# Reordered first loads, later decay tables, halved last sums and two-step sums of squares in a hybrid decoder layer

## The chip, the cores and the metric

The kernel runs on one core of a Trainium2 chip. The metric is device time in microseconds (us) of one execution. The core has five engines with their own instruction queues: TensorE (PE in the profile, with its weight loads shown apart as PEld), VectorE (DVE), ScalarE (ACT), GpSimd (POOL) and SyncE (SP), which here only issues DMAs. Each engine runs its queue in order; semaphores hold an instruction until what it depends on is done.

## The reference, cut to what matters

One decoder layer on x of shape (1, 1024, 1024), float32:

```python
xn   = rmsnorm(x, attn_norm_g)
proj = xn @ w_in                       # q, k, v of groups A and B, forget logits
qa, ka = rmsnorm(qa, q_norm_a), rmsnorm(ka, k_norm_a)       # per head of 64
out_a  = sliding_window_attention(qa, ka, va, sinks)        # 8 heads on 2 kv heads, window 128, ALiBi
qb, kb = rmsnorm(qb, q_norm_b), rmsnorm(kb, k_norm_b)
out_b  = forgetting_attention(qb, kb, vb, log_sigmoid(f + b_forget))   # 8 heads, causal
h = x + concat(out_a, out_b) @ w_out
y = h + relu(rmsnorm(h, mlp_norm_g) @ w_up) ** 2 @ w_down   # 4096 hidden
```

## The kernel before, in words

Everything is float32. A product of two float32 matrices is made of three matmuls in a faster float32 mode: each operand is split into a high part (a rounded copy, on ACT or DVE) and a low part (operand minus high part, on DVE or POOL; helper `split`, lines 74 to 79), and high·high, high·low and low·high are summed in PSUM. All matmuls come from the helper `mm` on line 72, so they share that line in the profile.

**Start (lines 166 to 204).** x comes transposed, 128 rows of it per step k = 0..7, each in two DMAs of 512 columns into `xr` (lines 177 and 181). The step's weights come as `wr`, 192 KB (line 178): by SP's queue, only for k = 0 by ACT's queue. DVE casts `wr` to the high part (line 78), DVE (k = 0) or POOL makes the low part (line 79); ACT scales x into `xh` (line 184), DVE makes `xl` (line 185). PE sums 24 products per step into eight PSUM banks `qps`, one per token tile t; the results are copied to `q0` by DVE (even t) and ACT (odd t) on line 203. Eight matmuls on a zero tile run before the first real one. `xr` has four buffers, shared later with `xq`; `wr` has three.

**Decay tables.** `ab` (lines 390 to 405) holds slope times distance for the 8 heads of group A: eight DVE multiplications of 128x256 of the tile `dist`, which POOL makes. They stand late in the program but need only `dist`, so they can be placed early in DVE's queue. They are read by the first scores of group A (line 506).

**Norms.** The second copy of x, `xq`, is squared and summed on ACT (line 379) for the row norms, which DVE and ACT turn into `rstd`, `ep2` and `rqk` (lines 380 to 385 with the helper `rsqrt`, lines 81 to 91). `qknorm` (lines 236 to 277) normalises queries and keys: POOL squares up to 1024 columns (line 244), one DVE instruction sums groups of 64 (line 249), small DVE and ACT steps make the factor (lines 254 to 269), POOL multiplies it in (line 275). It runs 14 times: ten with 16 groups, four with 12.

**Attention, then the two feed-forward products.** Projections of the next heads are matmuls that fill PE between scores (lines 501 to 510 and 652 to 661), transposed probabilities (`evict_pt`, lines 364 to 371: ACT makes `pth`, DVE then `ptl`) and sums with v. The feed-forward products use a seven-product scheme on half matrices; the loop `down` (lines 1124 to 1175) ends with product n = 2, whose four banks d = 0..3 are finished by DVE (lines 1226 and 1227: multiply by `rr`, add to a stored sum) and stored by SP one by one (line 1228).

**What sets the order.** A planner orders each engine's queue: it runs a cost model of the program in time and at each step issues, per engine, the ready instruction of the highest priority (program order, raised by `tc.high_priority(offset)` for `prep`, `load_w` and others). `tc.issue_after(ins)` adds one rule: what the block traces on `ins`'s engine is queued behind `ins`. Dependences between engines are kept by semaphores that the planner's framework sets per tile.

Of the kernel before, what the change touches and what calls it, by code (L numbers as in the profile page):

```python
# [12 lines left out]
ALU = mybir.AluOpType  # L13
# [3 lines left out]
P = 128  # L17
# [4 lines left out]
HD = 64  # L22
NH = 8
# [10 lines left out]
NU = 4  # L34
NS = 4
DEPTH = 2

LAST = (6, 7, 0, 1, 2, 3, 4, 5)
ORDER_B = (0, 2, 1, 3)
# [15 lines left out]
def hybrid_layer(  # L55
# [15 lines left out]
    def mm(out, lhsT, rhs, start, stop):  # L71
        return nc.tensor.matmul(out, lhsT, rhs, start=start, stop=stop)  # L72
# [101 lines left out]
    for k in range(KT):  # L174
        xr = ap2.tile([P, S], F32, tag="s", name="xr", bufs=NS)
        wr, wh, wl = w_tiles(384)
        nc.sync.dma_start(xr[:, halves[0]], xT[k * P : (k + 1) * P, halves[0]])
        (nc.sync if k else nc.scalar).dma_start(wr, w_a0[:, k, :])
        if k == 0:
            nc.scalar.preload_act_table_set("natural_log_exp_and_others")  # L180
        nc.sync.dma_start(xr[:, halves[1]], xT[k * P : (k + 1) * P, halves[1]])
        split(wh, wl, wr, nc.vector, nc.gpsimd if k else nc.vector)
        for cs in halves:
            nc.scalar.activation(xh[:, k, cs], xr[:, cs], AF.Copy, scale=ga[:, k : k + 1])
            nc.vector.scalar_tensor_tensor(
                out=xl[:, k, cs], in0=xr[:, cs], scalar=ga[:, k : k + 1],
                in1=xh[:, k, cs].bitcast(F32), op0=ALU.mult, op1=ALU.subtract,
            )
        passes = ((xh, wh), (xh, wl), (xl, wh))
        order = (  # L190
            [(t, j) for j in range(3) for t in range(NT)] if k == 0
            else [(t, j) for t in (range(NT) if k < KT - 1 else LAST) for j in range(3)]
        )
        for t, j in order:
            x_, w_ = passes[j]
            mm(
                qps[t][:, :384], x_[:, k, t * P : (t + 1) * P], w_,
                k == 0 and j == 0, k == KT - 1 and j == 2,
            )
# [36 lines left out]
    def qknorm(x, nh, tlo, thi, r=None):  # L236
# [9 lines left out]
            ap3.tile([P, 16], F32, tag=tag, name=tag, bufs=2)[:, : n * nh]  # L246
            for tag in ("ss", "sr0", "su")
        )
        nc.vector.tensor_reduce(
            out=ss, in_=sq[:, : n * w].rearrange("p (g d) -> p g d", d=HD),  # L250
            axis=AX.X, op=ALU.add,
        )
        th = lambda a: a.rearrange("p (t h) -> p t h", h=nh)
        nc.vector.scalar_tensor_tensor(
            out=th(ss), in0=th(ss), scalar=1.0 / HD,
# [145 lines left out]
        out=dist, in_=dist, pattern=[[1, 256]], compare_op=ALU.is_ge, fill=BIG,  # L401
        base=-1, channel_multiplier=-1,
    )
    for h in range(NH):
        nc.vector.tensor_scalar_mul(ab[h // 4][:, h % 4, :], dist, 2.0 ** -(h + 1))

    before = cp.tile([NH * NT, NH, NT], F32, name="before")
    nc.gpsimd.memset(before, 1.0)
# [715 lines left out]
    def down(i):  # L1124
# [8 lines left out]
        for ci in range(2):  # L1133
# [26 lines left out]
            for n in products:  # L1160
# [5 lines left out]
                split(w[:, 0], w[:, 1], src[n], nc.scalar, nc.vector if own else nc.gpsimd)  # L1166
                for d in range(4):
                    ds_ = slice(d * P, (d + 1) * P)
                    for k in range(2):
                        first, end = g + ci + k == 0, (g, ci, k) == (NG - 1, 1, 1)  # L1170
                        mm(ps[d], w[:, 0, k, ds_], x[:, 0, k], first, False)
                        mm(ps[d], w[:, 0, k, ds_], x[:, 1, k], False, False)
                        mm(ps[d], w[:, 1, k, ds_], x[:, 0, k], False, end)
                if (g, ci) == (NG - 1, 1):
                    finish(n, ps)

# [26 lines left out]
    def finish(n, ps):  # L1203
# [6 lines left out]
        for d in range(4):  # L1210
# [8 lines left out]
            elif n == 4:  # L1219
                plus(t[:, d], ps[d], sums["m7"][:, d])  # L1220
            elif n == 5:
                for name in ("m16", "m7"):
                    minus(sums[name][:, d], sums[name][:, d], ps[d])
            else:
                y = sums["m1"][:, d]
                nc.vector.tensor_tensor(out=ps[d], in0=ps[d], in1=rr[:, left], op=ALU.mult)
                plus(y, ps[d], y)
                nc.sync.dma_start(yT[d * P : (d + 1) * P, left], y)
        if n == 5:
            late.extend([("c21", 4, left), ("m7", 4, right), ("m16", 0, right)])  # L1230
        elif n == 3:
# [77 lines left out]
```

## Time and profile before

| | |
|---|---|
| time, median of 3 runs | 1115.2 us (1113.52 to 1115.54) |
| the profiled execution's own time | 1111.68 us |
| its span, first to last instruction | 1110.0 us |
| PE busy | 98% |
| DVE busy | 69% |
| ACT busy | 52% |
| POOL busy | 33% |
| mean granted TensorE clock | 0.999 of full speed |

A busy share is time in which at least one instruction of the engine ran. Matmuls are pipelined, so the distance between the starts of two of them (their pitch) is what one costs, and it is shorter than the duration shown. The end of a matmul is modelled.

### The profile page before, as it was taken

The numbers are of one execution on the slowest core, as the hardware profiler recorded it, in microseconds if no ns is written. First come the engines' busy times: TensorE is split into PE (matmuls) and PEld (weight loads), VectorE is DVE, ScalarE is ACT, GpSimd is POOL, SyncE is SP. The second block draws the span as 40 slices with busy tenths as digits, with TensorE's granted clock in tenths as the row PEclk, the third lists the DMA queues.
The fourth block names the chain that finished last, engine by engine and source line by source line (L and its number), as shares of the span: only waits on it lengthen the run. The fifth ranks groups of instructions, "written<-read, shape, count | busy, mean of one in ns | idle before, by whom it ended". The sixth has DMA issues, their size and how long they took to land.

```text
span 1110.0 us, 15616 instructions
## 1 busy us (share of the span) xinstructions
PE 1087.6 (98%) x5551; PEld 934.2 (84%) x5551; DVE 770.4 (69%) x1311; ACT 573.1 (52%) x1013; POOL 361.6 (33%) x338
## 2 busy tenths in 40 slices
PE   8999998999999999999999999999999999999998
PEld 7999987799997888787888888888888888888886
DVE  7476656765767477799868688756675877674395
ACT  5557657757667666555454535353443433333331
POOL 4662512424434655124322223322222222222100
PEclk9999999999999999999999999999999999999999
DMA  9301211304538566473554544334699786665423
GB/s 303 137 28 46 85 35 43 105 15 140 181 103 321 180 204 225 158 253 131 185 198 172 186 165 171 142 133 180 250 391 344 275 300 238 218 230 198 172 95 114
DMA packets 95935, 195.69 MB, mean 176 GB/s; under 512 B 7360, under 2 KB 19312, under 8 KB 95856
## 3 DMA queue, kind: packets, MB, share of 16 engines
q1 hardware_dynamic: 95568, 194.47, 49.9%
q8 instruction: 44, 0.72, 0.3%
q14 instruction: 35, 0.29, 0.1%
q10 hardware_dynamic: 288, 0.22, 0.1%
HBM read 141.61 MB, written 53.04 MB: 175 GB/s over the span
## 4 chain that ended last, share of the span: by engine, by line
PE 82%; DVE 9%; DMA 3%; issue 3%; ACT 2%; POOL 1%; SPq 0%; DVEq 0%; ACTq 0%; POOLq 0%
PE pd L72 27%; PE pu L72 26%; PE ps L72 12%; PE po L72 5%; PE spb L72 3%; PE pvb L72 3%; PE tpb L692 2%; PE sp L72 1%; DMA xq<-in_x_dram 1%; DVE ptl L368 1%; PE pv L72 1%; PE tpa L527 1%; DVE bl L79 1%; DVE sb L656 1%; DVE bl L918 1%
## 5 line engine op out<-in xcount | busy, mean ns | idle before, releaser
L72 PE MATMUL pd<-hx,wx 128*128 128x512 f32 x1344 | 304.8, 389 | 0.0
L72 PEld LDWEIGHTS pd<-hx,wx 128*128 128x128 f32 x1344 | 252.3, 188 | 52.4
L72 PE MATMUL pu<-bh,wu 128*128 128x512 f32 x896 | 276.6, 390 | 0.4 <-ACT wu L76 0.4
L72 PEld LDWEIGHTS pu<-bh,wu 128*128 128x128 f32 x896 | 168.2, 188 | 36.0 <-ACT wu L76 0.8
L72 PE MATMUL pu<-bl,wu 128*128 128x512 f32 x448 | 174.4, 390 | 0.8 <-DVE bl L79 0.8
L72 PE MATMUL ps<-w,xh 128*128 128x384 f32 (+1 forms) x640 | 173.4, 342 | 0.3 <-ACT qkb L609 0.3
L76 ACT CAST hx<-hr 128x1024 fp32r<-128x1024 f32 x56 | 59.0, 1054 | 175.8 <-PE pd L72 171.2
L79 POOL TENSOR_TENSOR wx<-wda,wx 128x1024 fp32r<-128x1024 f32 x24 | 64.4, 2684 | 196.5 <-ACT wx L76 188.1
L79 DVE TENSOR_TENSOR hx<-hr,hx 128x1024 fp32r<-128x1024 f32 x56 | 72.4, 1302 | 74.0 <-ACT hx L76 74.0
L72 PEld LDWEIGHTS ps<-w,xh 128*128 128x128 f32 x640 | 114.9, 189 | 1.3 <-ACT qkb L609 0.6
L72 PE MATMUL ps<-w,xl 128*128 128x384 f32 (+1 forms) x320 | 109.0, 341 | 0.0
L72 PEld LDWEIGHTS pu<-bl,wu 128*128 128x128 f32 x448 | 84.1, 188 | 18.9 <-DVE bl L79 1.4
L72 PE MATMUL po<-mix,wos 128*128 128x512 f32 x384 | 95.5, 396 | 0.7 <-ACT wos L76 0.7
L79 POOL TENSOR_TENSOR wu<-wus,wu 128x512 fp32r<-128x512 f32 x32 | 48.1, 1506 | 127.0 <-ACT wu L76 127.0
L72 PEld LDWEIGHTS po<-mix,wos 128*128 128x128 f32 x384 | 69.9, 188 | 14.5 <-ACT wos L76 1.1
L79 POOL TENSOR_TENSOR wu<-wur,wu 128x512 fp32r<-128x512 f32 x32 | 43.5, 1361 | 87.1 <-ACT wu L76 87.1
L368 DVE TENSOR_TENSOR ptl<-tpb,pth 128x512 fp32r<-128x512 f32 (+1 forms) x80 | 50.1, 633 | 29.8 <-ACT pth L367 29.2
L76 ACT CAST wu<-wus 128x512 fp32r<-128x512 f32 x64 | 38.4, 618 | 58.5 <-PE pu L72 56.0
L79 POOL TENSOR_TENSOR w<-wr,w 128x384 fp32r<-128x384 f32 (+1 forms) x47 | 50.0, 1079 | 49.3 <-ACT w L76 36.5
L987 DVE TENSOR_TENSOR ht<-hb 128x512 f32<-128x512 f32 x32 | 21.8, 722 | 63.4 <-ACT hb L1042 63.4
L76 ACT CAST wx<-wda 128x1024 fp32r<-128x1024 f32 x56 | 58.5, 1050 | 7.0 <-DMA wda<-in_w_d_dram 7.0
L367 ACT CAST pth<-tpb 128x512 fp32r<-128x512 f32 (+1 forms) x80 | 43.2, 544 | 34.7 <-PE tpb L692 30.1
(214 smaller groups left out, 1951.4 us busy)
## 6 DMA issues: line engine op xcount, KB each, us to landing
wda<-in_w_d_dram SPq DMA_DIRECT2D x34, 1024.0 KB, 8.8
hr<-hid_d SPq DMA_DIRECT2D x56, 512.0 KB, 6.1
wur<-in_w_u_dram SPq DMA_DIRECT2D x32, 512.0 KB, 4.3
hid_d<-ht SPq DMA_DIRECT2D x16, 1024.0 KB, 4.3
hid_d<-hb SPq DMA_DIRECT2D x16, 768.0 KB, 3.6
mix<-mixs_d SPq DMA_DIRECT2D x7, 1024.0 KB, 7.7
wr<-in_w_b_dram SPq DMA_DIRECT2D x32, 192.0 KB, 2.5
xr<-in_xT_dram SPq DMA_DIRECT2D x16, 256.0 KB, 4.3
```

The source lines that it names most:

```text
L72: return nc.tensor.matmul(out, lhsT, rhs, start=start, stop=stop)
L76: hi_eng.copy(hi, src)
L79: lo_eng.tensor_tensor(out=lo, in0=src, in1=hi.bitcast(F32), op=ALU.subtract)
L367: nc.scalar.copy(hi[:, cols], pt[:, cols])
L368: nc.vector.tensor_tensor(out=lo[:, cols], in0=pt[:, cols], in1=hi[:, cols].bitcast(F32), op=ALU.subtract)
L527: nc.tensor.transpose(tp[:, hh * P : (hh + 1) * P], pts[hh // 2][:, hh % 2, c0 : c0 + P], ident)
L656: nc.vector.tensor_tensor_reduce(out=pr[:, c * 512 : c * 512 + n], in0=sp[:, :n], in1=cb[:, c * 512 : c * 512 + n], scale=1.0, scalar=3e38 ...
L692: nc.tensor.transpose(tp[:, c0 : c0 + P], probs[qi][:, kb * P : (kb + 1) * P], ident)
L918: nc.vector.scalar_tensor_tensor(out=lo, in0=src, scalar=gain, in1=hi.bitcast(F32), op0=ALU.mult, op1=ALU.subtract)
L987: eng.tensor_tensor(out=out, in0=a, in1=b, op=ALU.subtract)
```

## The change

Four edits. The weights of step 0 are issued on SP's queue as its first DMA, ahead of the first half of x, instead of on ACT's queue behind `vecs`; the load of ACT's function table follows in the program. The eight decay-table multiplications are queued on DVE behind the last `xl` of the start. In `qknorm` the sum over groups of 64 is made by two DVE instructions, each on half of the groups. In the last group of products (n = 2, last step, d = 3) the six matmuls of 512 columns become twelve of 256, all six of the left half first, and DVE's multiply, add and the store of d = 3 are done per half.

```diff
+LAST_CS = (slice(0, 256), slice(256, 512))
...
         wr, wh, wl = w_tiles(384)
+        if k == 0:
+            nc.sync.dma_start(wr, w_a0[:, k, :])
+            nc.scalar.preload_act_table_set("natural_log_exp_and_others")
         nc.sync.dma_start(xr[:, halves[0]], xT[k * P : (k + 1) * P, halves[0]])
-        (nc.sync if k else nc.scalar).dma_start(wr, w_a0[:, k, :])
-        if k == 0:
-            nc.scalar.preload_act_table_set("natural_log_exp_and_others")
+        if k:
+            nc.sync.dma_start(wr, w_a0[:, k, :])
         nc.sync.dma_start(xr[:, halves[1]], xT[k * P : (k + 1) * P, halves[1]])
...
-            nc.vector.scalar_tensor_tensor(
+            last_x = nc.vector.scalar_tensor_tensor(
                 out=xl[:, k, cs], in0=xr[:, cs], scalar=ga[:, k : k + 1],
...
-        nc.vector.tensor_reduce(
-            out=ss, in_=sq[:, : n * w].rearrange("p (g d) -> p g d", d=HD),
-            axis=AX.X, op=ALU.add,
-        )
+        sqg = sq[:, : n * w].rearrange("p (g d) -> p g d", d=HD)
+        m = n * nh // 2
+        for g in (slice(0, m), slice(m, 2 * m)):
+            nc.vector.tensor_reduce(out=ss[:, g], in_=sqg[:, g], axis=AX.X, op=ALU.add)
...
-    for h in range(NH):
-        nc.vector.tensor_scalar_mul(ab[h // 4][:, h % 4, :], dist, 2.0 ** -(h + 1))
+    with tc.issue_after(last_x.ins):
+        for h in range(NH):
+            nc.vector.tensor_scalar_mul(ab[h // 4][:, h % 4, :], dist, 2.0 ** -(h + 1))
...
-                    for k in range(2):
-                        first, end = g + ci + k == 0, (g, ci, k) == (NG - 1, 1, 1)
-                        mm(ps[d], w[:, 0, k, ds_], x[:, 0, k], first, False)
-                        mm(ps[d], w[:, 0, k, ds_], x[:, 1, k], False, False)
-                        mm(ps[d], w[:, 1, k, ds_], x[:, 0, k], False, end)
+
+                    for cs in LAST_CS if (n, g, ci, d) == (2, NG - 1, 1, 3) else (slice(0, 512),):
+                        for k in range(2):
+                            first = g + ci + k == 0
+                            end = (g, ci, k) == (NG - 1, 1, 1) and cs.stop == 512
+                            mm(ps[d][:, cs], w[:, 0, k, ds_], x[:, 0, k, cs], first, False)
+                            mm(ps[d][:, cs], w[:, 0, k, ds_], x[:, 1, k, cs], False, False)
+                            mm(ps[d][:, cs], w[:, 1, k, ds_], x[:, 0, k, cs], False, end)
...
-                y = sums["m1"][:, d]
-                nc.vector.tensor_tensor(out=ps[d], in0=ps[d], in1=rr[:, left], op=ALU.mult)
-                plus(y, ps[d], y)
-                nc.sync.dma_start(yT[d * P : (d + 1) * P, left], y)
+                for cs in LAST_CS if d == 3 else (left,):
+                    y, p_ = sums["m1"][:, d, cs], ps[d][:, cs]
+                    nc.vector.tensor_tensor(out=p_, in0=p_, in1=rr[:, cs], op=ALU.mult)
+                    plus(y, p_, y)
+                    nc.sync.dma_start(yT[d * P : (d + 1) * P, cs], y)
```

## Rows read from the trace of the kernel before

**Rows 1.** The view of busy time by stretch of the span: stretch, its length, then busy us of PE, PEld, DVE, ACT and POOL with their instructions, the granted clock, the DMA engines' busy share and GB/s.

```profile
0.00:10.00 10.00, 6.84 (x27) 4.32 (x28) 6.80 (x23) 4.85 (x6) 4.20 (x16) 1.00 0.81 276
10.00:20.00 10.00, 10.00 (x59) 10.00 (x58) 10.00 (x14) 6.99 (x10) 5.74 (x5) 1.00 0.95 303
20.00:30.00 10.00, 10.00 (x60) 10.00 (x59) 4.24 (x6) 5.92 (x10) 4.87 (x5) 1.00 0.98 339
...
120.00:200.00 80.00, 74.00 (x450) 66.55 (x448) 48.87 (x138) 52.48 (x140) 28.02 (x27) 1.00 0.22 66
```

**Rows 2.** The timeline of the first 8 us, by engine: start us, us, engine, line, operation, out<-in, count, and in brackets the idle time before it with what ended it.

```profile
0.80 0.38 SPq L177 DMA_DIRECT2D xr<-in_xT_dram  x1
1.24 0.45 ACTq L178 DMA_DIRECT2D wr<-in_w_a_dram  x1
4.22 0.72 ACT L184 ACTIVATE xh<-xr,vt 128x512 fp32r<-128x512 f32 x1 [1.22 <-DMA vt<-in_vecs_dram]
5.24 0.72 ACT L184 ACTIVATE xh<-xr,vt 128x512 fp32r<-128x512 f32 x1 [0.30 <-DMA xr<-in_xT_dram]
4.63 1.70 DVE L405 TENSOR_SCALAR ab<-dist 128x256 f32<-128x256 f32 x8
6.25 0.35 DVE L78 CAST w<-wr 128x384 fp32r<-128x384 f32 x1
6.75 0.77 PE L72 MATMUL qps<-w,xh 128*128 128x384 f32 x3 [1.87 <-DVE w L78]
```

**Rows 3.** The view of DMA issues over the whole span: out<-in, queue, count, KB each, median us from issue to landing.

```profile
wr<-in_w_a_dram ACTq DMA_DIRECT2D x1, 192.0 KB, 4.1
wr<-in_w_b_dram SPq DMA_DIRECT2D x32, 192.0 KB, 2.5
...
mix_d<-mta SPq DMA_DIRECT2D x32, 64.0 KB, 1.7
...
out_dram<-m SPq DMA_DIRECT2D x4, 256.0 KB, 2.0
```

**Rows 4.** The timeline between the row norms and the first scores, columns as in rows 2.

```profile
37.07 0.17 DVE L380 TENSOR_SCALAR rt<-rt 128x8 f32<-128x8 f32 x1 [12.55 <-ACT xq L379]
38.61 0.96 DVE L87 TENSOR_TENSOR u<-u,rt 128x8 f32<-128x8 f32 x1
40.43 1.01 DVE L203 COPY q<-qps 128x384 f32<-128x384 f32 x2
41.12 1.90 POOL L244 TENSOR_TENSOR sq<-q 128x1024 f32<-128x1024 f32 x1 [1.57 <-DVE q L203]
43.05 1.22 DVE L249 TENSOR_REDUCE ss<-sq 128x16 f32<-128x1024 f32 x1 [1.61 <-POOL sq L244]
46.68 1.21 DVE L249 TENSOR_REDUCE ss<-sq 128x16 f32<-128x1024 f32 x1
48.42 0.22 DVE L424 SCALAR_TENSOR_TENSOR z<-ps,rstd,vt 128x8 f32<-128x8 f32 x1
...
56.99 0.95 DVE L249 TENSOR_REDUCE ss<-sq 128x12 f32<-128x768 f32 x1
57.98 0.74 DVE L289 SCALAR_TENSOR_TENSOR q1a<-ptq,gqk,q1a 64x512 fp32r<-64x512 f32 x1
58.78 0.38 PE L72 MATMUL sp<-k1a,q1a 128*128 128x256 f32 x1 [0.41 <-DVE q1a L289]
```

**Rows 5.** The view of groups with shapes kept apart: line, engine, operation, out<-in, shapes, count, then busy us, mean ns of one, and idle time before.

```profile
L249 DVE TENSOR_REDUCE ss<-sq 128x16 f32<-128x1024 f32 x10 | 12.2, 1216 | 3.1 <-POOL sq L244 3.0
...
L249 DVE TENSOR_REDUCE ss<-sq 128x12 f32<-128x768 f32 x4 | 3.8, 950 | 1.3 <-POOL sq L244 1.3
```

**Rows 6.** The timeline at two later places where a sum of squares stands in DVE's queue, columns as in rows 2.

```profile
197.90 0.59 ACT L367 CAST pth<-tpa 128x512 fp32r<-128x512 f32 x1
...
198.60 1.22 DVE L249 TENSOR_REDUCE ss<-sq 128x16 f32<-128x1024 f32 x1
...
200.47 0.63 PE L296 MATMUL ptk<-ident,qkb 128*64 128x128 f32 x4 [1.43 <-DVE ptl L368]
...
338.00 0.59 ACT L367 CAST pth<-tpb 128x512 fp32r<-128x512 f32 x1
...
339.13 1.21 DVE L249 TENSOR_REDUCE ss<-sq 128x16 f32<-128x1024 f32 x1
...
341.00 0.39 PE L72 MATMUL pvb<-ptl,vb 128*128 128x256 f32 x1 [1.72 <-DVE ptl L368]
```

**Rows 7.** The chain of waits over the last 30 us: start us, us, what.

```profile
1082.91 18.37 PE pd L72 x81
```

**Rows 8.** The timeline of DVE at the very end, columns as in rows 2: the add for d = 2, then the multiply and the add for d = 3.

```profile
1104.77 0.69 DVE L990 TENSOR_TENSOR m<-pd,m 128x512 f32<-128x512 f32 x1
1105.39 0.70 DVE L1226 TENSOR_TENSOR pd<-pd,rr 128x512 f32<-128x512 f32 x1
1106.13 0.69 DVE L990 TENSOR_TENSOR m<-pd,m 128x512 f32<-128x512 f32 x1
```

**Rows 9.** The timeline at a group of scores, columns as in rows 2: the first and the last of four matmuls into one bank (the first two write its left half), and DVE's read of the left half.

```profile
105.55 0.28 PE L72 MATMUL sp<-k1a,q1a 128*128 128x256 f32 x1
...
105.90 0.28 PE L72 MATMUL sp<-k2z,q1a 128*128 128x256 f32 x1
106.22 0.48 DVE L506 CUSTOM_DVE_ANT_0 sa<-sp,ab,nsnk 128x256 f32<-128x256 f32 x1
```

## The prediction

> **What bounds the kernel now.** The busy times on the page come first: PE works 98% of the span and no other engine over 69%, so time is won only where PE stands idle or where the ends of the span, which PE doesn't fill, get shorter. The view by stretch shows where that is: PE is busy 6.84 of the first 10 us, all of the next 20, and idle again in the attention stage, for instance 6.0 of the 80 us from 120 on [rows 1]. The change touches three such places: the start, sums of squares on DVE before and inside the attention stage, and the last stores. The timeline of the first 8 us shows the start: PE waits 1.87 us for the first weights' high part, which DVE casts at 6.25, directly behind eight decay-table multiplications that began at 4.63 and hold DVE for 1.70 us [rows 2]. The end is PE's last products, then DVE's multiply and add for the last bank and its store [rows 7, 8]. The timeline from 37 to 59 us shows what PE meets after its unbroken start: the first scores wait 0.41 us for DVE's q1a, at the end of a chain of POOL and DVE work [rows 4].
>
> **Sums against the profiled execution.** It took 1111.68 us with a span of 1110.0. The median of the runs shown is 1115.2, 3.5 above it. All terms below are differences, taken off the median. About 0.2%, 2.2 us, is what a measurement of this kernel can tell from no change.
>
> **Start: weights first, tables later.** Removed ahead of the cast: 1.70 us of tables. When can the cast run then? Before, the weights were issued at 1.24 on ACT's queue and landed 4.1 us later, at 5.34 [rows 2, 3]. Issued first on SP's queue at 0.80, they land between 3.3 (2.5 us, the median of the same size from SP in a later stage) and 4.9 (4.1 us). DVE's small steps on `vecs` end at 4.7, just before the tables began, so the cast starts at 4.7 to 5.34 instead of 6.25. The first half of x is now issued one DMA later. Its `xh` ran at 4.22, when `vecs` had landed [rows 2]. With 192 KB ahead of it, 0.6 us at the 303 GB/s of the next stretch [rows 1], I take 4.5, so `xh` is there at 5.2. A matmul began 0.15 us after the cast's end before (6.60 to 6.75). So PE begins at 5.35, that is 1.4 earlier; with the late landing at 5.85, 0.9 earlier; at best 1.5. The second half of x was awaited until 5.24 and that total of bytes is unchanged, so its `xh` is done near 6.0 and PE reaches it at 6.07: no new stall worth counting. On SP's queue, all later DMAs are issued 0.44 us later at first; on ACT's the table load comes 0.44 earlier, ahead of a wait for `vecs` that ends later anyway. The tables cost nothing at their new place: behind the last `xl` DVE sat idle 12.55 us until the row norms at 37.07 [rows 4], which holds 1.70 easily, and the scores read them at 58.78 or later. Without that cover the 1.70 would stand in front of the norms.
>
> How much of 1.4 reaches the first scores? PE isn't what set them: q1a ended at 58.72 on a chain back through the norms (46.68, 43.05), POOL's square at 41.12, which waited for DVE's copies of q0 at 40.43, and `xq`, whose last sum let DVE start at 37.07 [rows 4]. `xq` is loaded behind x and two weight blocks while the DMA engines are 0.95 to 0.98 busy [rows 1]: an earlier issue can't land much earlier, 0 to 0.5 us. The copies depend on PE, but the row-norm steps stand between them on DVE (one of 0.96 us, at 38.61). If the planner lets the copies go first, the square starts up to 1.3 earlier; if not, by what `xq` gains. PE itself meets the chain first at 48.42 (z must empty a PSUM buffer), then at 58.78. Ends: 0 and 1.4 kept; both ways out are about as near, so I take half, **-0.7**.
>
> **Sums of squares in two steps.** Fourteen more DVE instructions. The two sizes give (1.216 - 0.950)/256 = 1.04 ns per column and 0.15 us fixed [rows 5], so a half of 512 columns takes 0.68 and two take 1.37 end to end. At the end of the kernel DVE began an independent multiply 0.07 before the add ahead of it ended (1105.39 against 1105.46) [rows 8]; with that the pair takes 1.30, 0.08 more than one sum. Its ends are 0 and 0.15 more. Three of the sums lie on the chain to the first scores: +0.24. Against that, work may slip between the halves. At 56.99 a sum of 0.95 stands before q1a, for which PE waits: up to 0.4 less. At 198.60 and 339.13 a sum of 1.22 starts after `pth` was there (198.49 and 338.59), and PE waits 1.43 and 1.72 us for the `ptl` that DVE makes behind the sum [rows 6]: up to 0.55 less each, if the planner sees `ptl` ready when the first half ends. In its model the sum was the better choice once, so I count half of each. In the other sums I see no PE wait. +0.24 - 0.2 - 0.55 is **-0.5**, between +0.8 (0.08 for each of ten sums that meet PE, nothing slips in) and -1.5.
>
> **The last sums by halves.** Matmuls of 512 columns follow each other at 18.37/81 = 0.227 us [rows 7]; those of 256 at (105.90 - 105.55)/3 = 0.117 [rows 9]. Twelve cost 1.40 instead of 1.36, so PE ends at 1105.41 instead of 1105.37 (d = 0 ended at 1101.28, plus eighteen at 0.227). But DVE isn't free before: d = 2 kept it until 1105.39, when the multiply for d = 3 began; multiply to add took 0.74, and the add ended at 1106.82 [rows 8]. With 0.27 less per half (256 columns at 1.04 ns), the four instructions start 0.47, 0.35 (0.70 less 0.07 and 0.27) and 0.47 apart and the last takes 0.42: 1.71 in place of 1.43, an end 0.28 later. The last store shrinks from 256 to 128 KB: 2.0 us for 256 and 1.7 for 64 KB [rows 3] make 1.8, 0.2 less. Net +0.1.
>
> A wait is added too. In the trace DVE began to read a score bank's left half only at 106.22, after all four matmuls into that bank had been issued, the last at 105.90 with 0.28 [rows 9], although the left half's two were through by about 105.95. So the left half of d = 3 will wait for PE's right half as well: 1105.41 plus the 0.04 that rows 9 show between a matmul's end and DVE's start, against 1105.39 where DVE comes free, 0.06 later. The halves then don't overlap PE at all, and the term is **+0.2** (from -0.2, should the store gain 0.5, to +0.6). The Trainium skill says why this is not an accident (PSUM — Partial Sum Buffer, "PSUM bank collisions raise a hardware error"): two engines mustn't touch one bank in the same partitions at once, disjoint columns included, so they are kept apart by bank, not by address. By it the tail is +0.2; could halves overlap, it would be +0.1; rows 9 agree with the rule.
>
> **Sum.** -0.7 - 0.5 + 0.2 = -1.0: 1114.2 us.
>
> **Rivals.**
> *Faster: the whole start arrives and sums let others through.* For it: PE runs without a break from 10 to 30 us [rows 1], so it keeps its lead that long, and the planner fills PE by readiness. Against it: DMA at 0.95 and more. -1.4 (start) - 1.5 (all that can slip in) + 0.2 = -2.7, and if a unit of the idle 6 us in 120 to 200 falls out with the new order, more: about 1111.9.
> *Slower: late factors before the first scores.* The second half of a sum can be put behind other ready work, and the factor needs both. Place: the sums at 43.05, 46.68 and 56.99, the one chain without slack. Price: a split like q1a's, 0.74, in each, 2.2 in all, with 0.24 for the halves, +0.2 for the tail, and the start lost behind it: +2.6, 1117.8. It decides once the chain is later by more than the 1.4 by which PE leads plus its 0.41 of wait. For it: the stretch has other work for DVE between the sums (z, q1a) [rows 4]; against it: the norms of the later tiles carry raised priority.
> *No effect: the first edit doesn't do what it says.* DMA and the norm chain set the first scores as before, the 1.4 is spent in the waits at 48.42 and 58.78, and -0.2 from sums meets +0.2 at the tail: 1115.2.
>
> **How the numbers follow.** The forecast of -1.0 has 0.40, with its own range 1113.0 to 1115.6 (start at either end, sums half way to theirs); faster 0.27; slower 0.20; no effect 0.13. Faster by over 0.2%, under 1113.0: the rival's 0.27 and 0.08 of the forecast, **0.35**. Slower, over 1117.4: nearly all of its rival and a little of reordering anywhere, **0.21**. Within: **0.44**. The range, leaving a tenth on either side, is 1110.7 to 1118.0: the faster rival with about 1 us of reordering beyond it, and the slower one.
>
> **What would show it.** Start: the first real matmul at 5.2 to 5.9 in place of 6.75, the tables on DVE after 22 us. Chain: POOL's first square before 41.1 and the first scores before 58.78, by about 0.7. Sums: 28 of them, 0.68 and 0.55 us long; a `ptl` between halves at the two places and PE's waits there near 0.9 and 1.2. Tail: twelve matmuls 0.117 apart, DVE's four steps over 1.7 us and none before the twelfth matmul is issued. I'm wrong if PE's waits between 60 and 460 us change by more than 2 us: then the planner's new order, not these terms, sets the time.

## The result, and the profile after

The changed kernel takes 1118.52 us (median of 15 runs, 1116.19 to 1120.74). The kernel before, run beside it on the same chip, takes 1114.63 (15 runs, 1111.3 to 1118.69). The ratio is 1.0039, with a 95% interval of 1.0027 to 1.005: slower by about 4 us, where 1114.2 and a range up to 1118.0 were forecast. The profiled execution of after took 1120.74 us, the longest of its 15, with a span of 1119.0; that of before, 1111.68, lay near its shortest. The two traces are 9 us apart, and more than half of that is the spread from run to run. So a difference between them counts below only where other traces repeat it; before, after and the experiments make seventeen traces.

The busy times of after's page are the shares of before, to a per cent: PE 98%, DVE 69%, ACT 51 instead of 52%, POOL 33%. Four microseconds don't show in an average over the span; they have to be looked for by place.

```profile
PE 1092.5 (98%) x5557; PEld 936.1 (84%) x5557; DVE 772.8 (69%) x1327; ACT 573.3 (51%) x1013; POOL 364.3 (33%) x338
```

**The start** is what was forecast. The timeline of after's first 8 us (columns as in rows 2; line numbers of after are one to eight higher) has the cast of the weights at 3.77 in place of 6.25, `xh` at 4.55 and PE's first matmul at 5.33, where rows 2 have 6.75.

```profile
3.77 0.36 DVE L79 CAST w<-wr 128x384 fp32r<-128x384 f32 x1 [1.23 <-DMA wr<-in_w_a_dram]
...
4.55 0.72 ACT L187 ACTIVATE xh<-xr,vt 128x512 fp32r<-128x512 f32 x1 [2.03 <-DMA xr<-in_xT_dram]
...
5.33 3.40 PE L73 MATMUL qps<-w,xh 128*128 128x384 f32 x16 [0.45 <-ACT xh L187]
```

Nothing of the 1.42 us is left at the first scores, which start at 59.34 in place of 58.78. The same timeline between the norms and the scores, beside [rows 4]: the first sum starts 0.43 later than before, the third 0.51, and PE waits 1.00 us for q1a in place of 0.41. That the scores come later at all is not shown: in the seventeen traces they start between 58.30 and 60.75.

```profile
43.48 1.28 DVE L255 TENSOR_REDUCE ss<-sq 128x8 f32<-128x512 f32 x2 [1.53 <-POOL sq L247]
...
57.50 1.01 DVE L255 TENSOR_REDUCE ss<-sq 128x6 f32<-128x384 f32 x2
58.54 0.74 DVE L292 SCALAR_TENSOR_TENSOR q1a<-ptq,gqk,q1a 64x512 fp32r<-64x512 f32 x1
...
59.34 0.39 PE L73 MATMUL sp<-k1a,q1a 128*128 128x256 f32 x1 [1.00 <-DVE q1a L292]
```

**The sums.** In the view of groups with shapes kept apart, the 14 sums of rows 5 are 28, and each is as long as forecast (0.68 and 0.55). The timeline above shows a pair as one row of 1.28, against 1.22 for the single sum: 0.06 more.

```profile
L255 DVE TENSOR_REDUCE ss<-sq 128x8 f32<-128x512 f32 x20 | 12.8, 680 | 3.5 <-POOL sq L247 3.4
...
L255 DVE TENSOR_REDUCE ss<-sq 128x6 f32<-128x384 f32 x8 | 4.0, 547 | 1.3 <-POOL sq L247 1.3
```

At the two places of rows 6 no `ptl` slipped between the halves. At the first the pair stands together, and PE waits 1.49 where it waited 1.43. At the second an `mtb` went between them, and PE waits 1.78 where it waited 1.72.

```profile
202.14 1.28 DVE L255 TENSOR_REDUCE ss<-sq 128x8 f32<-128x512 f32 x2
203.34 0.68 DVE L371 TENSOR_TENSOR ptl<-tpa,pth 128x512 fp32r<-128x512 f32 x1
...
204.07 0.63 PE L299 MATMUL ptk<-ident,qkb 128*64 128x128 f32 x4 [1.49 <-DVE ptl L371]
...
342.54 0.68 DVE L255 TENSOR_REDUCE ss<-sq 128x8 f32<-128x512 f32 x1
343.25 0.42 DVE L714 TENSOR_TENSOR mtb<-pvb,tmpb 64x256 f32<-64x256 f32 x1
343.70 0.69 DVE L255 TENSOR_REDUCE ss<-sq 128x8 f32<-128x512 f32 x1
...
345.64 0.38 PE L73 MATMUL pvb<-ptl,vb 128*128 128x256 f32 x1 [1.78 <-DVE ptl L371]
```

**The tail** costs nothing that shows: from the end of PE's last matmul to the end of the span it is 4.62 us in both traces, and 4.62 or 4.63 in all seventeen. The timeline of DVE at the end answers to rows 8: the multiply of the left half starts at 1114.45, 0.04 after PE's last matmul into the right half has ended (34 of them from 1107.83 on, 6.58 long), and the four steps stand 0.46 to 0.47 apart.

```profile
1107.83 6.58 PE L73 MATMUL pd<-hx,wx 128*128 128x512 f32 x34
...
1114.45 0.43 DVE L1234 TENSOR_TENSOR pd<-pd,rr 128x256 f32<-128x256 f32 x1
1114.91 0.42 DVE L994 TENSOR_TENSOR m<-pd,m 128x256 f32<-128x256 f32 x1
1115.37 0.43 DVE L1234 TENSOR_TENSOR pd<-pd,rr 128x256 f32<-128x256 f32 x1
1115.84 0.42 DVE L994 TENSOR_TENSOR m<-pd,m 128x256 f32<-128x256 f32 x1
```

**Two new places.** Near 130 us PE stands still for 2.07 us. The timeline there reads upwards: PE waits for `pth`, ACT makes `pth` behind a cast of weights, the cast has waited 3.92 us for `wr`, and `wr` stands on SP's queue behind a load of `mixr`, issued at 126.40 when the stores to `mix_d` had landed. In before that load was issued at 123.79, the cast waited 2.47 us and PE 0.62.

```profile
126.40 0.32 SPq L580 DMA_DIRECT2D mixr<-mix_d  x1
126.82 1.54 SPq L218 DMA_DIRECT2D wr<-in_w_b_dram  x3
...
130.04 0.51 ACT L77 CAST w<-wr 128x384 fp32r<-128x384 f32 x1 [3.92 <-DMA wr<-in_w_b_dram]
130.83 0.59 ACT L370 CAST pth<-tpa 128x512 fp32r<-128x512 f32 x1
...
131.47 0.50 PE L73 MATMUL pv<-pth,va 128*128 128x512 f32 x1 [2.07 <-ACT pth L370]
```

The same timeline of before:

```profile
123.79 0.32 SPq L576 DMA_DIRECT2D mixr<-mix_d  x1
...
125.65 2.29 SPq L215 DMA_DIRECT2D wr<-in_w_b_dram  x3
...
128.04 0.52 ACT L76 CAST w<-wr 128x384 fp32r<-128x384 f32 x1 [2.47 <-DMA wr<-in_w_b_dram]
...
129.48 0.50 PE L72 MATMUL pv<-pth,va 128*128 128x512 f32 x1 [0.62 <-ACT pth L367]
```

The later issue is only a part of it. The first `wr` is issued 3.96 us after the first of the stores in place of 3.49 (the stores start at 122.86, in before at 122.16), and the cast starts 3.22 us after that issue in place of 2.39. Then the load of `mixr` and those of `wr` are under way together; that this is why `wr` takes longer is not shown.

The view by stretch (columns as in rows 1) shows what followed: the granted clock is 0.58 and 0.57 in the next two stretches, so PE ran at 1.2 GHz for most of them.

```profile
130.00:132.00 2.00, 0.53 (x3) 0.49 (x4) 0.95 (x5) 1.96 (x5) 1.37 (x2) 1.00 0.25 66
132.00:134.00 2.00, 2.00 (x11) 2.00 (x10) 1.32 (x3) 2.00 (x9) 2.00 (x2) 0.58 0.62 209
134.00:136.00 2.00, 2.00 (x8) 2.00 (x8) 1.44 (x4) 1.10 (x5) 2.00 (x3) 0.57 0.57 204
```

The second place is at 440.69, where PE waits 1.40 us for a `ptl` (0.60 in before, at 433.95). It is taken up with the experiments.

```profile
440.69 0.39 PE L73 MATMUL pvb<-ptl,vb 128*128 128x256 f32 x1 [1.40 <-DVE ptl L371]
```

### The profile page after: what moved, and what is told of

The parts are those of the page before. It is cut to its first block, busy times and chain, and to the rows that moved or that the text cites. A ratio compares the mean times of both kernels' runs of the same rounds, so it can differ in the third digit from the quotient of the medians.

```text
span 1119.0 us, 15649 instructions
## 1 busy us (share of the span) xinstructions
PE 1092.5 (98%) x5557; PEld 936.1 (84%) x5557; DVE 772.8 (69%) x1327; ACT 573.3 (51%) x1013; POOL 364.3 (33%) x338
## 4 chain that ended last, share of the span: by engine, by line
PE 83%; DVE 8%; DMA 4%; issue 2%; ACT 2%; POOL 1%; SPq 0%; DVEq 0%; ACTq 0%; POOLq 0%
PE pd L73 27%; PE pu L73 26%; PE ps L73 11%; PE po L73 5%; PE spb L73 3%; PE qps L73 2%; PE pvb L73 2%; PE tpb L696 2%; PE sp L73 1%; DVE ptl L371 1%; PE pv L73 1%; PE tpa L531 1%; DVE ss L255 1%; DMA wr<-in_w_b_dram 1%; DMA rr<-part_d 1%
## 5 line engine op out<-in xcount | busy, mean ns | idle before, releaser
L73 PE MATMUL pd<-hx,wx 128*128 128x512 f32 (+1 forms) x1350 | 304.9, 388 | 0.0
L80 POOL TENSOR_TENSOR wx<-wda,wx 128x1024 fp32r<-128x1024 f32 x24 | 69.5, 2895 | 191.4 <-ACT wx L77 191.4
L73 PEld LDWEIGHTS ps<-w,xl 128*128 128x128 f32 x320 | 60.7, 190 | 0.5
```

Of the source, the lines that this page charges most:

```text
L80: lo_eng.tensor_tensor(out=lo, in0=src, in1=hi.bitcast(F32), op=ALU.subtract)
```

## The experiments

All sets were run beside the kernel before, which had medians of 1114.1, 1113.96, 1114.18 and 1114.29 us in the four of them. The table has the results; the expectations below it were written before the runs.

| kernel | median us | runs | ratio to before (95% interval) |
|---|---|---|---|
| e1_start_only | 1114.62 | 12 | 1.0006 (0.9996 to 1.0017) |
| e2_two_step_only | 1118.64 | 5 | 1.0048 (1.0035 to 1.0061) |
| e3_halves_only | 1114.07 | 11 | 1.0002 (0.9991 to 1.0012) |
| e4_all_but_two_step | 1113.47 | 12 | 1.0000 (0.9991 to 1.0008) |
| f1_only_12th_sum | 1116.79 | 12 | 1.0024 (1.0015 to 1.0032) |
| f2_copy_before_12th_sum | 1117.0 | 9 | 1.0027 (1.0017 to 1.0037) |
| f3_one_group_before_12th_sum | 1114.05 | 12 | 1.0000 (0.9992 to 1.0009) |
| f4_eleven_of_fourteen | 1113.39 | 12 | 1.0000 (0.999 to 1.0011) |
| g1_mix_load_later | 1113.75 | 11 | 1.0000 (0.9992 to 1.0009) |
| g2_two_step_mix_load_later | 1117.32 | 6 | 1.0031 (1.002 to 1.0043) |
| g3_thirteen_not_12th | 1115.83 | 11 | 1.0011 (1.0001 to 1.002) |
| g4_thirteen_not_7th | 1116.69 | 8 | 1.0025 (1.0015 to 1.0036) |
| h1_12th_multiply_earlier | 1115.07 | 12 | 1.0003 (0.9994 to 1.0012) |
| h2_multiply_earlier | 1114.83 | 11 | 1.0003 (0.9995 to 1.0012) |
| h3_multiply_and_load | 1114.53 | 11 | 1.0003 (0.9994 to 1.0012) |

### Which of the edits costs

**e1_start_only** has the first two edits (weights first, tables later).

```diff
+        if k == 0:
+            nc.sync.dma_start(wr, w_a0[:, k, :]); nc.scalar.preload_act_table_set("natural_log_exp_and_others")
         nc.sync.dma_start(xr[:, halves[0]], xT[k * P : (k + 1) * P, halves[0]])
...
+    with tc.issue_after(last_x.ins):
+        for h in range(NH): nc.vector.tensor_scalar_mul(ab[h // 4][:, h % 4, :], dist, 2.0 ** -(h + 1))
```

> First weights ahead on SP's queue and tables behind the last xl; sums of squares and last sums as before. The order of every engine is that of the kernel before, but for the first 60 instructions or so. Theory A (the new order that the two-step sums give the attention stage costs the time): -0.5 us against before (0 to -1.4), first real matmul at 5.3, no stretch of lower granted clock near 130 us. Theory B (the start itself costs: PE's lead turns into longer waits and the clock falls): +2 to +5 us.

**e2_two_step_only** has the third.

```diff
+        for g in (slice(0, m), slice(m, 2 * m)):
+            nc.vector.tensor_reduce(out=ss[:, g], in_=sqg[:, g], axis=AX.X, op=ALU.add)
```

> Only the sums of squares in two steps. Theory A: all of the loss is here, +4 us (+3 to +6), the same wait of some 2 us for pth near 130 us with a lower granted clock behind it. Theory B: +0.3 (four times 0.08) or less.

**e3_halves_only** has the fourth.

```diff
+                    for cs, k in [(cs, k) for cs in (LAST_CS if (n, g, ci, d) == (2, NG - 1, 1, 3) else (slice(0, 512),)) for k in range(2)]:
...
+                for cs in LAST_CS if d == 3 else (left,):
...
```

> Only the last sums by halves. Both theories: +0.2 us (-0.2 to +0.6); DVE's end 0.3 later after PE's last product, the store's 0.2 shorter.

**e4_all_but_two_step** has all but the third.

```diff
+            nc.sync.dma_start(wr, w_a0[:, k, :]); nc.scalar.preload_act_table_set("natural_log_exp_and_others")
...
+    with tc.issue_after(last_x.ins):
...
+                for cs in LAST_CS if d == 3 else (left,):
...
```

> The changed kernel with the sums of squares in one step again. Theory A: -0.3 us against before, so some 4 us faster than the changed kernel. Theory B: +2 to +5, as the changed kernel.

Measured: the two steps alone lose 4.5 us, everything else nothing beyond the intervals (for e1 up to 1.9 us, for e3 and e4 about 1 us either way). In e4 PE's first matmul comes at 4.88, 1.87 earlier than in before, and the first scores at 58.60, 0.18 earlier; in e1 they come at 58.94, 0.16 later. So the start's lead ends at the norms. Theory A holds, and what it says can be seen in the built queues: start and halves move instructions only at the two ends, while the two-step sums put PE's queue in another order over most of the attention stage (some hundreds of lines of difference, from instruction 337 to 2762).

### Which sum, and whether it is the sum at all

In the queues that the planner builds, splitting most of the fourteen one at a time moves next to nothing. The twelfth (273.85 us in before) moves more than 300 lines of PE's queue behind it. The fourteenth by itself moves about a hundred, the seventh fewer than twenty. **f1_only_12th_sum** splits the twelfth (`calls` counts the calls of `qknorm`):

```diff
-        nc.vector.tensor_reduce(
-            out=ss, in_=sq[:, : n * w].rearrange("p (g d) -> p g d", d=HD),
-            axis=AX.X, op=ALU.add,
-        )
+        sqg = sq[:, : n * w].rearrange("p (g d) -> p g d", d=HD); calls.append(0)
+        m = n * nh // 2
+        for g in (slice(0, m), slice(m, 2 * m)) if len(calls) == 12 else (slice(0, 2 * m),):
+            nc.vector.tensor_reduce(out=ss[:, g], in_=sqg[:, g], axis=AX.X, op=ALU.add)
```

> Only the twelfth of the fourteen sums of squares (at 273.85 us in the trace of before) is made in two steps; all else is as before. It is the one call whose split alone changes the order of the rest of the attention stage: 328 lines of PE's queue, the same as with all fourteen split from there on. Theory A (the new order behind this one sum costs): about +2.2 us, ratio 1.0020, since the trace of e2_two_step_only lost 3.2 us between the first ptk<-ident,qkb (184.6 before) and the last pvb<-ptl,vb (455.0 before) where three kernels with the old order lost 0.6 to 1.3. The loss then shows as a later last pvb against the first ptk by some 2 us. Theory B (each second instruction costs its share, 4.5 us over 14): +0.3 us, ratio 1.0003. Theory C (the whole loss is the wait and the half clock near 130 us, which belongs to the seventh sum): 0, ratio 1.0000, and no loss between 270 and 460 us.

**f2_copy_before_12th_sum** splits none (the sum itself stands on one line here). It adds a copy of one column ahead of the twelfth sum, which then overwrites it.

```diff
+        if len(calls) == 12:
+            nc.vector.tensor_copy(ss[:, :1], sqg[:, :1, 0])
         nc.vector.tensor_reduce(out=ss, in_=sqg, axis=AX.X, op=ALU.add)
```

> All fourteen sums in one step as before; ahead of the twelfth stands one more DVE instruction, a copy of a single column into a number that the sum overwrites at once. Its queues are those of f1_only_12th_sum, instruction for instruction on PE, ACT, POOL and SP. Theory A (order): as f1_only_12th_sum within 0.5 us, about +2.2 us, ratio 1.0020, though no sum is split. Theory B (the two steps themselves): +0.1 us for the copy, ratio 1.0001. Theory C (half clock near 130 us): 0.

**f3_one_group_before_12th_sum** adds a sum over one group at the same place.

```diff
+        if len(calls) == 12:
+            nc.vector.tensor_reduce(out=ss[:, :1], in_=sqg[:, :1], axis=AX.X, op=ALU.add)
         nc.vector.tensor_reduce(out=ss, in_=sqg, axis=AX.X, op=ALU.add)
```

> As f2_copy_before_12th_sum, but the added DVE instruction is a sum over a single group of 64 into the number that the full sum overwrites. With it the queues of PE differ from before in 66 lines only and are the old ones again from instruction 1975 of PE on. Theory A (order): 0 to +0.5 us, ratio 1.0000 to 1.0005, since nearly all of the old order stands, and so clearly under f2_copy_before_12th_sum, though the instruction added is longer. Theory B (more DVE work before the factor): +0.2 us, at least as much as f2_copy_before_12th_sum. Theory C: 0.

**f4_eleven_of_fourteen** splits all but the seventh, twelfth and fourteenth.

```diff
+        for g in (slice(0, m), slice(m, 2 * m)) if len(calls) not in (7, 12, 14) else (slice(0, 2 * m),):
```

> Eleven of the fourteen sums are made in two steps, all but the seventh, twelfth and fourteenth, whose splits move the order. PE's queue differs from before in 12 lines. Theory A and C (order behind the twelfth, wait near 130 us behind the seventh): +0.2 us at most, ratio 1.0000 to 1.0002. Theory B (each second instruction costs its share): 11/14 of 4.5 us, +3.5 us, ratio 1.0032.

Measured: the split of one sum loses 2.8 us (1116.79 against 1113.96), and a copy of one column that leaves every sum whole loses 3.0; the longer instruction of f3 (0.21 us, the copy 0.14) loses nothing, and eleven split sums lose nothing. Theory B falls: the price is not in the instructions. f1 and f2 share their queues on PE, ACT, POOL and SP and share their time. The instructions that f2 and f3 add differ by a trifle and their times by 3 us; what sets them apart is the order, since f3's queue on PE is the old one again from instruction 1975 on. It is the order behind the twelfth sum that costs. Theory C falls as the whole reason, since f1 and f2 lose without a long wait near 130 us.

### The wait near 130 us

**g1_mix_load_later** leaves all sums whole and puts the load of `mixr`, which nobody reads before 250 us, behind the weights.

```diff
-            nc.sync.dma_start(wr, src[:, k, :])
+            wloads.append(nc.sync.dma_start(wr, src[:, k, :]))
...
-                nc.sync.dma_start(m, mix_d[e][:, cs])
+                with tc.issue_after(wloads[-1].ins): nc.sync.dma_start(m, mix_d[e][:, cs])
```

> No sum is split. The two first loads of mixr, which wait for the landing of mix_d's stores and are used from 250 us on, stand behind the weights wr on SP's queue instead of ahead of them; every other queue is that of before, instruction for instruction. In the profiled executions of before the first of them is issued 1.6 us after the stores, in those of e1_start_only, e2_two_step_only and after 3.5 us after; then wr lands late, PE idles 2.0 to 2.3 us near 130 us and its granted clock is 0.5 for 3.41 us after it. Theory D (this wait, by chance in half of the runs of the old order and in nearly all of the new one, is the part of the loss that is not the order behind the twelfth sum): -0.5 to -1.0 us against before, ratio 0.9992, no wait over 1 us near 130 us, and less spread. Theory E (the half clock comes anyway, at another wait): 0, ratio 1.0000.

**g2_two_step_mix_load_later** is the same on top of e2's edit.

```diff
+                with tc.issue_after(wloads[-1].ins): nc.sync.dma_start(m, mix_d[e][:, cs])
...
+        for g in (slice(0, m), slice(m, 2 * m)):
+            nc.vector.tensor_reduce(out=ss[:, g], in_=sqg[:, g], axis=AX.X, op=ALU.add)
```

> All fourteen sums in two steps, and the first loads of mixr behind the weights as in g1_mix_load_later; the other queues are those of e2_two_step_only. Theory D: the 2.0 us wait near 130 us and the half clock behind it are gone and the rest of the loss is that of the twelfth sum: +2.5 us against before, ratio 1.0022, 2 us under e2_two_step_only. Theory E: as e2_two_step_only, +4.0 us, ratio 1.0036, with a half clock elsewhere.

**g3_thirteen_not_12th** and **g4_thirteen_not_7th** each leave one sum whole.

```diff
+        for g in (slice(0, m), slice(m, 2 * m)) if len(calls) != 12 else (slice(0, 2 * m),):
```

> All sums in two steps but the twelfth. PE's queue differs from before in 114 lines, most of them behind the fourteenth sum. With the order behind the twelfth out, theory A and D: what is left of the 4.5 us is the share of the wait near 130 us and whatever the fourteenth sum's order does: +0.5 to +1.5 us, ratio 1.0009. Theory A alone (the twelfth is all of it): 0, ratio 1.0000. Theory B (the pairs themselves), which f4_eleven_of_fourteen already spoke against: +4.2 us.

```diff
+        for g in (slice(0, m), slice(m, 2 * m)) if len(calls) != 7 else (slice(0, 2 * m),):
```

> All sums in two steps but the seventh. Its queues differ from e2_two_step_only by 8 lines of PE and 2 of ACT, between 111 and 131 us: the cast of a weight block that waits for wr stands behind two exponentials again instead of ahead of one of them. Theory F (this seat of the cast on ACT makes the wait near 130 us certain): the loss falls to that of the twelfth sum alone, +2.7 us, ratio 1.0024, and half or more of the runs show a mean clock of 0.999 or more. Theory D without F (the landing of the stores alone decides, not ACT's order): as e2_two_step_only, +4 us, ratio 1.0036.

Measured: g3 loses 1.65 us in the medians and 1.2 by its ratio, g4 2.5. Together with f1 the sum closes as far as intervals of about 1 us either way can tell: without the twelfth 1.2 is left, without the seventh 2.5, and 1.0011 and 1.0024 make 1.0035, beside 1.0039 for after. g3 also has the fourteenth sum's order, so its 1.2 is not by itself that of the wait near 130 us. The traces part the two. From the first matmul `ptq<-ident,qkb` (173.72 us in before) to the last `pvb<-ptl,vb` (455.04) g3 takes 282.31 us, and the seven traces of the old order without a stretch of low clock there, g3 counted, take 281.32 to 282.61: the fourteenth shows no price. Ahead of that, from the first scores on, g3 takes 116.26 us, where the thirteen traces with the short wait take 114.82 to 115.76, and after, e1 and e2, with the half clock behind the long wait, 117.87 to 118.21. The timelines of g3 and g4 differ near 130 us. In g3, which splits the seventh sum, the load of `mixr` is issued 3.6 us after the stores (124.12), and PE waits 2.09 us:

```profile
124.12 0.80 SPq L543 DMA_DIRECT2D mix_d<-mta  x2
127.73 0.32 SPq L576 DMA_DIRECT2D mixr<-mix_d  x1
...
132.75 0.50 PE L72 MATMUL pv<-pth,va 128*128 128x512 f32 x1 [2.09 <-ACT pth L367]
```

In g4, which leaves it whole, it is issued 1.6 us after them, and PE waits 0.66:

```profile
122.55 0.80 SPq L543 DMA_DIRECT2D mix_d<-mta  x2
124.18 0.32 SPq L576 DMA_DIRECT2D mixr<-mix_d  x1
...
129.90 0.50 PE L72 MATMUL pv<-pth,va 128*128 128x512 f32 x1 [0.66 <-ACT pth L367]
```

Of the fourteen traces that have this load in its old place, the long gap stands in e2, g3 and after, which split the seventh sum, and in e1; the other ten, none of which splits it, have the short one. That supports theory F, as g4's time does; but ACT's seat of the cast can't be the only reason, since e1 has the long gap with the old seat. How the long gap begins, the view of DMA issues from 118 to 130 us says (columns as in rows 3): the stores land later. In before:

```profile
mix_d<-mta SPq DMA_DIRECT2D x2, 64.0 KB, 2.2
```

and in after:

```profile
mix_d<-mta SPq DMA_DIRECT2D x2, 64.0 KB, 3.4
```

Why they land later there stays open. Taking the load out of the way cures the wait where it occurs: in g2 PE waits 0.57 us near 130 and the median falls from 1118.64 to 1117.32, 1.3 of the 2 that theory D expected, in another set and with intervals that overlap. In g1 it gains nothing (theory E): in these traces the old order has the wait once, in e1.

### The wait near 437 us

What in the order behind the twelfth sum takes the time? PE's waits in f1, read against before, differ most at 436.72, and three timelines explain that row. In f1, POOL adds two `pc` blocks to `xt` one behind the other, DVE's multiply into `mixr` starts beside them and takes 1.42 us, and the `ptl` that PE waits for is behind it:

```profile
432.99 2.52 POOL L860 TENSOR_TENSOR xt<-xt,pc 128x512 f32<-128x512 f32 x2
...
434.64 1.42 DVE L586 TENSOR_TENSOR mixr<-mixr,mixn 128x512 f32<-128x512 f32 x1
435.99 0.68 DVE L368 TENSOR_TENSOR ptl<-tpb,pth 128x512 fp32r<-128x512 f32 x1
...
436.72 0.38 PE L72 MATMUL pvb<-ptl,vb 128*128 128x256 f32 x1 [1.40 <-DVE ptl L368]
```

In before one addition ends as the multiply starts, and it takes 0.67:

```profile
431.41 1.28 POOL L860 TENSOR_TENSOR xt<-xt,pc 128x512 f32<-128x512 f32 x1 [0.67 <-ACT pc L859]
...
432.62 0.67 DVE L586 TENSOR_TENSOR mixr<-mixr,mixn 128x512 f32<-128x512 f32 x1
433.22 0.68 DVE L368 TENSOR_TENSOR ptl<-tpb,pth 128x512 fp32r<-128x512 f32 x1
...
433.95 0.39 PE L72 MATMUL pvb<-ptl,vb 128*128 128x256 f32 x1 [0.60 <-DVE ptl L368]
```

After has the same at 438.61: a multiply of 1.42 and a wait of 1.40 at 440.69. **h1_12th_multiply_earlier** adds to f1's edit: it keeps f1's order up to there and queues that multiply behind an earlier `ptl`.

```diff
-        nc.vector.tensor_tensor(
+        ptls.append(nc.vector.tensor_tensor(
             out=lo[:, cols], in0=pt[:, cols], in1=hi[:, cols].bitcast(F32), op=ALU.subtract
-        )
+        ).ins)
...
-            with tc.issue_after(mixed[-1]):
+            with tc.issue_after(ptls[-1] if (e, c) == (6, 0) else mixed[-1]):
```

> As f1_only_12th_sum (only the twelfth sum in two steps), but the multiply into mixr that runs at 434.64 us there is queued earlier on DVE, behind the ptl of 429.5, ahead of a stretch in which DVE sat idle for 2.25 us. PE's queue differs from f1_only_12th_sum in 20 lines, from its instruction 2661 on. Theory G (the multiply that meets POOL's addition holds up the ptl behind it): PE's wait for ptl at 436.7 falls from 1.40 to under 0.5 us and the time by 0.8 to 1.3 us against f1_only_12th_sum, to a ratio of 1.0014 against before. Theory H (the wait is filled by the next one; the loss is spread over the order): the time stays at that of f1_only_12th_sum, ratio 1.0024.

**h2_multiply_earlier** is that edit in the old order.

```diff
+            with tc.issue_after(ptls[-1] if (e, c) == (6, 0) else mixed[-1]):
```

> The old order, no sum split; the same multiply into mixr is queued earlier on DVE, as in h1_12th_multiply_earlier. In before it takes 0.67 us at 432.62 and PE waits 0.60 us for the ptl behind it. Theory G: PE's wait at 434 goes, -0.6 us, ratio 0.9995. Theory H: 0, ratio 1.0000.

**h3_multiply_and_load** adds g1's.

```diff
+                with tc.issue_after(wloads[-1].ins): nc.sync.dma_start(m, mix_d[e][:, cs])
...
+            with tc.issue_after(ptls[-1] if (e, c) == (6, 0) else mixed[-1]):
```

> The old order with both repairs, the multiply into mixr earlier and the first loads of mixr behind the weights. If both waits cost what the traces show: -0.6 us and -0.5 us against before, ratio 0.9990; if neither is worth anything by itself, as g1_mix_load_later (ratio 1.0000) already said of the loads: 1.0000.

Measured: h1 takes 1115.07, and its ratio of 1.0003 is that of the old order within its interval, while the twelfth sum is still split and its order stands up to PE's instruction 2661. The multiply takes 0.68 us there and PE's wait is 0.41:

```profile
432.77 0.68 DVE L586 TENSOR_TENSOR mixr<-mixr,mixn 128x512 f32<-128x512 f32 x1
...
438.62 0.39 PE L72 MATMUL pvb<-ptl,vb 128*128 128x256 f32 x1 [0.41 <-DVE ptl L368]
```

Theory G is right about the place and low on the price: against before, the time fell by 2.1 us in the medians and 2.3 by the ratios, the wait only by 1.0. The rest is not that wait. The view by stretch, from the first `ptq<-ident,qkb` to the last `pvb<-ptl,vb` (columns as in rows 1), shows first f1, then h1:

```profile
173.51:459.39 285.88, 274.76 (x1700) 241.27 (x1699) 188.53 (x465) 189.47 (x414) 116.33 (x158) 0.99 0.45 151
175.72:459.18 283.46, 274.07 (x1700) 241.16 (x1699) 188.39 (x465) 189.24 (x414) 116.98 (x158) 0.99 0.46 152
```

The same 1700 matmuls take 2.42 us less, and PE idles 9.39 us in place of 11.12. The clock is not the reason, since each of the two has one stretch of half clock there, of the same length: h1's from 343.73 on, f1's from 438.05 on, behind that wait. In f1:

```profile
436.00:438.00 2.00, 1.07 (x7) 0.83 (x7) 2.00 (x4) 0.79 (x2) 2.00 (x2) 1.00 0.83 322
438.00:440.00 2.00, 1.87 (x8) 1.87 (x9) 1.42 (x6) 0.30 (x1) 0.90 (x3) 0.51 0.86 290
```

Sorted by the clock, all traces say the same. With such a stretch, f1, f2 and g2, which have the order behind the split twelfth sum, take 285.25 to 285.99 us; f3, f4 and h2, which have the old one, 283.37 to 283.47, and h1 is among these. Without it, after, e2 and g4 take 284.35 to 284.58, the old order 281.32 to 282.61. So the order costs about 2 to 3 us at either clock, and in its trace h1 takes all of it back. Of h1's 2.42, PE's idle time is 1.73; why the busy time fell by the other 0.69 is open. The edit also changed the order of the last 100 instructions of the stage, which wasn't taken apart, so that the multiply alone gives the time back is likely and not shown; nor was the edit tried on the changed kernel itself. In the old order the edit is worth nothing (h2, h3): the multiply meets another `xt` addition at its new place and takes 1.69 us at 429.20, and what PE no longer waits for `ptl` it waits for `mix`. None of the fifteen beats the kernel before by more than can be measured.

## Why the prediction was wrong

**Start, -0.7.** The times that set PE's start were right: `xh` at 4.55 (4.5 forecast), PE at 5.33 (5.35). The cast came at 3.77, a microsecond ahead of its 4.7, which gained nothing, since PE then waited for `xh`. What failed is "I take half": in e1 and e4 nothing is kept that shows, though e4's interval (from 0.9991) would still hold the 0.7. The first scores are set by the norm chain, as the rival of no effect said, and PE's lead is spent in its waits: in e4 0.95 us for z at 48.52 and 0.41 for q1a.

**Sums in two steps, -0.5, with an end of +0.8: the step that failed.** It measures +4.5 alone (e2). Its parts: the pair costs 0.06 more (0.08 forecast), which is right and worthless. "Work may slip between the halves" was counted at -0.55 and gave nothing; in e2 and after 13 of the 14 pairs run back to back, and only an `mtb` stands in the last. "In the other sums I see no PE wait" was misread: PE waits 0.81 us for `ptl` at 277.10 in before, behind the twelfth. But not even that row has the price of its split, which lies 160 us further on: one more instruction at that place, a copy as well as a half (f2), turns choices of the planner until the end of the stage. Both ends of this term were worked out from the instructions beside the sums. A changed order was put at "about 1 us" on the fast side of the range and at "a little" of the chance of slower; as a term it was nothing. That it may outweigh all the others stood only in the last sentence, "then the planner's new order, not these terms, sets the time". That condition was met: from 60 to 460 us PE is busy for 384.90 of 400 us in after and 387.00 in before, so it idles 15.1 in place of 13.0 (15.05 in e2, 13.06 in e4).

**Last sums, +0.2.** Right to 0.2: e3 is at 1.0002, which can't tell 0.2 from 0, the tail behind PE is 4.62 us as before, and the left half did wait for PE's right half. DVE ends 0.4 later after PE, for the steps are 0.46 apart in the middle in place of 0.35, and the last store of 128 KB lands in 1.7 us, 0.3 less than the 256 KB before.

**The rivals.** The slower one named the sums at 43.05, 46.68 and 56.99. The three are not it: f4 splits them all and is at 1.0000. Its price of +2.6 came near by accident. The faster one needed the start to arrive, which it didn't, and work to slip between the halves, which one `mtb` did. The one of no effect was right about the start and put the sums at -0.2, where e2 measures +4.5.

So 1114.2 missed by 4.3 us: 0.7 for the start, 0.5 for gains at the sums, 0.2 back at the tail, 3.9 for an order that had no term, and 0.6 back because the base of 1115.2 was 1114.63 in fifteen runs. By f1 and g3 that 3.9 is about 2.7 behind the twelfth sum and 1.2 near 130 us, each to about 1 us.

## What to carry to other kernels

Where a planner orders the queues, one more instruction is a new order, and its first effect is not its own duration. Compare the built queues of the two kernels engine by engine before pricing anything: an edit that moves hundreds of lines needs a range as wide as other orders of the same work are apart, here 3 us. The count of moved lines is no price by itself: against before, f3 moved 66 lines of PE's queue and f4 twelve, for nothing, and h1 moved twenty of f1's and took 2 us off. And where an order costs, look for the single place in it, a wait that one moved instruction undoes, before blaming the edit.

## What the runs showed of the hardware

**DVE's multiply waits for POOL.** In the traces of before and f1, the 14 multiplies into `mixr` take 0.67 to 0.69 us when POOL runs nothing at their start. Those that start inside a two-input POOL instruction last until about 0.55 us after that instruction has ended, three of them in before and five in f1; a fourth in before met POOL only for its last 0.07 us and took its usual 0.67. One of the three:

```profile
286.08 1.45 DVE L586 TENSOR_TENSOR mixr<-mixr,mixn 128x512 f32<-128x512 f32 x1
...
285.67 1.30 POOL L79 TENSOR_TENSOR mixs<-mixr,mixn 128x512 fp32r<-128x512 f32 x1
```

POOL ended at 285.67 + 1.30 = 286.97 and the multiply at 286.08 + 1.45 = 287.53. The Trainium skill (SBUF — State Buffer, "SBUF: two separate sides") says that DVE and GpSimd share one pair of SBUF ports as an exclusive lock, which a DVE instruction with two SBUF inputs needs while a GpSimd instruction that reads SBUF holds it, and that the loser is blocked for the whole instruction. These rows agree but for 0.12 us: behind POOL's end the multiply still takes 0.55 us, and 0.67 alone. In the other traces it is the same 0.54 or 0.55 wherever POOL's instruction had 0.15 us or more left. They could have been read before the prediction.

A longer multiply doesn't cost time wherever it stands. In f1's order two others are longer as well, at 283.68 (1.35 us, 0.88 in before) and 318.54 (1.39 us); h1 keeps both, at 1.35 and 1.39, and has the old order's time.

**The clock falls behind some waits and not behind others.** PE ran at 1.2 GHz behind the wait of 2.07 us in after and behind the 1.40 us of f1, and stayed at 2.4 behind the 2.09 us of g3 (granted clock 1.00 in every stretch from 130 to 138 us). The wait at 341.00 in before (1.72 us) is in all traces (1.18 us in g3, 1.71 to 1.78 in the others), and a granted clock of 0.5 follows it in five of the seventeen: f3, f4, g2, h1 and h2. It differs from one execution to the next: of 115 runs of before beside the experiments, 49 had a mean clock of 0.998 or less and took 1115.0 us on average, the other 66 took 1113.7. In after it was 14 of 15 and in e2 5 of 5. That is about half of the runs more than in before, at 1.3 us each: by that estimate some 0.6 us of the 4 go with the clock.
